# Gated linear attention: scores per head over 64 rows of TensorE instead of per pair with zero-padded queries

## The chip, the cores and the metric

The kernel runs on one NeuronCore of a Trainium2 chip. The metric is the device time of one execution, in microseconds, as the median of several runs. The program is one launch that computes two whole layers of a hybrid block, with nothing done on the host in between. It is written with a tile framework: the code allocates tiles from pools, and a scheduler in the build decides, from its own model of time, in which order the instructions stand on each engine, and which physical buffer each tile takes. On the chip the engines then run their fixed orders and wait for each other through semaphores.

## The reference, cut to what is touched

Each layer mixes tokens with three groups of heads (retention, gated linear attention, RWKV-7), projects the result, and runs a feed-forward network. The change concerns gated linear attention (GLA) alone: 4 heads, 48 key channels (padded to 64 in the kernel), 96 value channels, chunks of 64 tokens, in both directions over 1024 latent and 256 context tokens.

```python
def _gla_scan(seq, s0):
    """Chunked gated linear attention: S_n = diag(alpha_n) S_{n-1} + k_n^T v_n, o_n = q_n S_n."""
    causal = jnp.tril(jnp.ones((CHUNK, CHUNK), dtype=bool))

    def step(s, blk):
        qb, kb, vb, gb = blk
        cum = jnp.cumsum(gb, axis=2)
        rel = cum[:, :, :, None, :] - cum[:, :, None, :, :]
        decay = jnp.exp(jnp.where(causal[:, :, None], rel, -jnp.inf))
        sc = jnp.einsum("bhid,bhjd,bhijd->bhij", qb, kb, decay)
        o = jnp.einsum("bhij,bhjv->bhiv", sc, vb) + jnp.einsum("bhid,bhdv->bhiv", qb * jnp.exp(cum), s)
        ...
```

The score of a query i and a key j in one chunk carries a decay for every channel between i and j. The kernel does not form the array over (i, j, d). It splits the 64 x 64 square of a chunk into seven levels: the diagonal, and for block lengths 32, 16, 8, 4, 2 and 1 the pairs in the two halves of a block of twice that length. For a pair of one level the decay is a product of a factor of the query and a factor of the key, both measured from the middle of the block, so each level is one matrix product; masks put the levels together.

## The kernel before

Channels lie on partitions. A pair t of heads (t = 0, 1) fills the 128 partitions: head e of the pair has partitions 64e to 64e+63. The stage works on blocks n of 128 tokens (two chunks r = 0, 1), ten of them in layer 0 and eight in layer 1, and is the generator `gla` (L1063). For each block it yields once:

- `front(n+1)` (L1095) loads the next block: `gk` (keys), `gqz` (queries), `gvg` (values and gate), `glr`, and computes the log decays `glah` + `glal`. The queries are loaded zero-padded, by two transfers of half the partitions: `gqz` is [128, pair, 2, 128], and in its slot e only the partitions of head e hold queries; the others stay zero from a memset (L1078).
- `scores(n)` (L1116), for each pair t: for each chunk r two 512-wide decay exponents through PSUM tiles `pg` into `gEX` (L1132, ScalarE), then `gQT` (L1136, VectorE: the six levels' query factors times the padded queries, 768 wide), the keys' factors (L1138, GpSimd), `gqe` (L1139) and `gkh` (L1141) on VectorE. Then come the products: for each level and each chunk one matmul whose stationary operand is the keys of both heads (128 rows, 64 columns) and whose moving operand is the padded queries of both heads (128 wide). The padding keeps the heads apart. Chunk r writes the partitions 64r to 64r+63 of a PSUM tile. Levels (diagonal, 0, 1, 2) go to one bank, levels (3, 4, 5) to a second (L1143 to L1153). After each bank, VectorE puts its levels together into `gsc`: one product for the diagonal (L1156), one masked copy for each other level (L1158).
- `back(n)` (L1161) uses `gsc`, `gqe` and the states for the outputs, and updates the state `gSf` (L1013).

All these PSUM tiles have the tag `g1`, with GB = 4 banks; `back` has one more bank, `g2`. The names of the profile drop the bank number: both read as `pg`. In a row of the profile a matmul in float32 stands as two records, each with its own weight load: 14 score matmuls of a pair are 28 records, 4 of them named `pg<-gqz,gk` (the diagonal) and 24 named `pg<-gQT,gEX`.

Other work is interleaved with the blocks: the retention mixer (`rr`, `qx`, `mu`, `y`), the modulation matmuls whose weights `wmod` come by transfer (`pn`), and beside the last three blocks of a layer the output projection (`rw`). All transfers are issued from SP's queue (L246), all matmuls by L243.

Of the kernel before, what the change touches and what calls it, by code (L numbers as in the profile page):

```python
# [35 lines left out]
GB = 4  # L36
# [33 lines left out]
def rw_where(u):  # L70
    """block and chunk of either direction in step u"""
    ns = [(0, 1), (1, 0)][u // 2] if u < 4 else (u // 2, 11 - u // 2)
    return [(ns[0], u % 2), (ns[1], 1 - u % 2)]
# [96 lines left out]
class Kern:  # L170
# [77 lines left out]
    # ------------------------------------------------------------------ setup  # L248
# [34 lines left out]
    # per layer vectors, channel-major, and modulation  # L283
# [18 lines left out]
    def mod(self, l, V, p, parts, bufs):  # L302
        """parts: which sixths of the modulation (1024 columns each) to compute"""
# [27 lines left out]
    def mod_gain(self, l, V, part_scale, gname, add_one):  # L331
        """per-partition gain [128, 8, 2] = g * (scale + 1) or g * scale"""
# [11 lines left out]
    # ------------------------------------------------------------ norms  # L344
    def rstd(self, x, b, dst, pe=False):
        """dst [128, N] = (mean over channels of x^2 + 1e-6) ** -0.5 on all partitions; x [128, 8, N]; pe: the tensor
        engine sums over the channel tiles too"""
# [26 lines left out]
    def split_norm(self, x, b, A, B, s, xh, xl, pe=False):  # L374
        """xh + xl = x * rstd * A + B, x [128, 8, N]; A, B [128, 8, 2]"""
# [12 lines left out]
    def resid(self, f, b, gp, s, xsrc, xdst, pe=False):  # L388
        """f <- x + gp * f * rstd(f), in place; xsrc DRAM [128, 8, TOK], xdst also, or [128, 8, SEQ]"""
# [22 lines left out]
    # ------------------------------------------------------------ dense helpers  # L412
    def weights(self, p, segs, width):
        """segs: list of (dst offset, DRAM AP [1024, w]); returns lists of the hi and lo parts [128, width] per k tile"""
# [38 lines left out]
    # ------------------------------------------------------------ P1: RWKV columns  # L453
# [176 lines left out]
    def rw_heads(self, t, e):  # L630
        """the heads of parity e"""
        return t.rearrange("p (j e) x -> p e j x", e=2)[:, e]
# [10 lines left out]
    def rw_row(self, l, i, t, back=False):  # L643
        """row i of the operands, of all chunks, from t (or back into t)"""
# [5 lines left out]
    def rw_load(self, l, P, X, u):  # L650
        """operands of step u into X [128, 2, 9 or 15, 64], the decays into P; returns the inverse decay, kk and kk a of
        either direction"""
# [18 lines left out]
    def rw_decayed(self, dst, ops, P):  # L671
        """kk times the decay up to the token before"""
# [3 lines left out]
    def rw_inverses(self, l, p):  # L676
        """the triangular matrices of all steps, and the inverses of their diagonal blocks of 32 x 32"""
# [25 lines left out]
    def rw_inverse(self, l, bi):  # L703
        """minus the inverse of (identity + triangular), 96 matrices of 32 x 32, one per partition, in place; then the
        operands of the solves, [rows, (step, head), inverse | factors of its block off the diagonal]"""
# [21 lines left out]
    def silu(self, p, o, x):  # L727
        """o = x / (1 + exp(-x)) by Exp and Ln"""
# [8 lines left out]
    # ------------------------------------------------------------ P1: GLA and retention columns  # L737
# [64 lines left out]
    # ------------------------------------------------------------ retention mixer  # L802
    def ret(self, l, ctx_out, p):
# [18 lines left out]
        def rot(dst, src, n):  # L822
            """axial rotary over [128, 4, 2, 2, 16]"""
# [20 lines left out]
        def upd(d, new, old, kh, v):  # L844
            """new = decay * old + khat^T v, [128 (2 heads x 64), (2, 64)]"""
# [129 lines left out]
    # ------------------------------------------------------------ gated linear attention mixer  # L975
# [8 lines left out]
    def gla_logsig(self, p, ps):  # L984
        """log_sigmoid(ps), [128, n]"""
# [37 lines left out]
    def gla_state(self, l, p, C, d, n, bank, nb=2):  # L1023
        """k-hat (transposed) and per-chunk decays for direction d, block n"""
# [17 lines left out]
    def gla_back(self, l, p):  # L1042
        """states of the backward direction in front of every chunk"""
# [19 lines left out]
    def gla(self, l, ctx_out, p):  # L1063
# [16 lines left out]
        def early():  # L1080
            return self.pt("g1", GB)

# [12 lines left out]
        def front(n):  # L1095
# [4 lines left out]
            for e in range(2):  # L1100
                self.dma(qz[64 * e:64 * e + 64, :, e, :], self.QK[l][64 * e:64 * e + 64, 0:2, 128 * n:128 * n + 128])
# [640 lines left out]
```

## Time and profile before

| | |
|---|---|
| runs of the kernel before | 4218.07, 4218.18 and 4226.98 us, median 4218.18 |
| span of the profiled execution | 4221.6 us (no other time is given for that execution) |
| GLA stage, layer 0 / layer 1 | about 905 to 1225 us / 3125 to 3377 us of that span |
| TensorE, VectorE, ScalarE, GpSimd busy over the span | 93%, 56%, 39%, 41% |
| records of score matmuls | 864 + 144 = 1008 |

The profile page gives busy times, the span in 40 slices, and the chain of work that ended last. The trace behind it answers by tile, by line, by window and in order of time. A matmul's recorded duration holds the time in which it drains, so TensorE's busy share overstates its load; how many matmuls follow each other in what time tells more.

### The profile page before, as it was taken

To read this page: it belongs to the slowest core of one execution; us is meant where nothing else is said; L and a number is where in the kernel's file an instruction comes from. 1 tells how busy PE (TensorE), PEld (TensorE's weight loads), DVE (VectorE), ACT (ScalarE), POOL (GpSimd) and SP (SyncE) were. 2 spreads that over 40 slices of the span, in tenths; PEclk is the share of its full clock that TensorE was granted. 3 is DMA by queue.
4 is the path that set the end of the run, shared out by engine and by line. 5 is a ranking of instruction groups with operands and counts; after the bars stand their busy time and mean duration, and the time that the engine had idled before them with its cause. 6 is when DMAs were issued, how large, how long until landed. Compare 5 with 4: busy or idle time off the path is not lost. (4 is left out here: it accounts for less than half of the span.)

```text
span 4221.6 us, 74050 instructions
## 1 busy us (share of the span) xinstructions
PE 3927.3 (93%) x29094; PEld 3157.3 (75%) x29094; DVE 2346.4 (56%) x4053; ACT 1629.1 (39%) x3267; POOL 1730.6 (41%) x1686
## 2 busy tenths in 40 slices
PE   7998999899999999999998997999888979999998
PEld 3776888776677788888885675887856757888886
DVE  4565656658756633644445464666658565335444
ACT  4442334234435333522224443343244344334332
POOL 3155630323456544522223145640423465445443
PEclk8998999899999999999998998999989989999999
DMA  6586545665433333322222387554764253334332
GB/s 191 129 235 183 140 125 146 191 186 184 126 120 112 108 92 106 97 65 60 61 60 92 86 225 202 129 148 135 206 196 122 66 157 96 99 94 134 93 97 93
DMA packets 822655, 547.18 MB, mean 130 GB/s; under 512 B 317853, under 2 KB 727201, under 8 KB 822305
## 3 DMA queue, kind: packets, MB, share of 16 engines
q1 hardware_dynamic: 822016, 541.38, 44.9%
q8 instruction: 229, 3.75, 0.4%
q14 instruction: 122, 0.99, 0.1%
q0 software_dynamic: 288, 1.05, 0.1%
HBM read 421.96 MB, written 120.33 MB: 128 GB/s over the span
## 5 line engine op out<-in xcount | busy, mean ns | idle before, releaser
L243 PE MATMUL pd<-xh,whi 128*128 128x512 f32 (+1 forms) x2608 | 981.8, 377 | 30.8 <-ACT whi L433 13.9
L434 POOL TENSOR_TENSOR wlo<-wraw,whi 128x1024 fp32r<-128x1024 f32 (+1 forms) x328 | 678.4, 2072 | 786.8 <-ACT whi L433 652.2
L243 PE MATMUL pd<-xl,whi 128*128 128x512 f32 (+1 forms) x2608 | 987.7, 379 | 12.4 <-DVE xl L1437 4.6
L243 PE MATMUL pd<-xh,wlo 128*128 128x512 f32 (+1 forms) x2608 | 982.5, 377 | 15.7 <-POOL wlo L434 15.7
L243 PEld LDWEIGHTS pd<-xh,whi 128*128 128x128 f32 x2608 | 500.3, 192 | 135.1 <-DVE xh L384 18.8
L243 PEld LDWEIGHTS pd<-xl,whi 128*128 128x128 f32 x2608 | 500.5, 192 | 122.9 <-issue 13.4
L243 PEld LDWEIGHTS pd<-xh,wlo 128*128 128x128 f32 x2608 | 500.6, 192 | 118.3 <-POOL wlo L434 20.5
L433 ACT CAST whi<-wraw 128x1024 fp32r<-128x1024 f32 (+1 forms) x328 | 289.2, 891 | 483.1 <-PE pd L243 266.9
L1517 DVE TENSOR_TENSOR f<-pm,f 128x512 f32<-128x512 f32 (+1 forms) x400 | 247.2, 635 | 354.1 <-PE pm L243 354.1
L1503 POOL TENSOR_TENSOR dl<-draw,dh 128x512 fp32r<-128x512 f32 x176 | 242.6, 1378 | 480.2 <-ACT dh L1502 450.8
L243 PE MATMUL pm<-hl,dh 128*128 128x512 f32 (+1 forms) x880 | 327.6, 373 | 8.1 <-DVE hl L1492 8.1
L243 PE MATMUL pm<-hh,dh 128*128 128x512 f32 (+1 forms) x880 | 322.3, 374 | 9.4 <-DVE f L1517 3.9
L243 PE MATMUL pd<-whi,xh 128*128 128x256 f32 x1072 | 317.6, 297 | 1.9 <-DVE st L438 1.9
L243 PE MATMUL pm<-hh,dl 128*128 128x512 f32 (+1 forms) x880 | 318.2, 372 | 0.0
L243 PE MATMUL pd<-wlo,xh 128*128 128x256 f32 x1072 | 317.8, 297 | 0.0
L243 PE MATMUL pd<-whi,xl 128*128 128x256 f32 x1072 | 317.7, 297 | 0.0
L1502 ACT CAST dh<-draw 128x512 fp32r<-128x512 f32 x176 | 109.1, 620 | 456.7 <-DMA draw<-in_w_ffn_down 245.1
L236 ACT ACTIVATE silu<-silu 128x512 f32<-128x512 f32 (+2 forms) x332 | 171.7, 517 | 191.9 <-DVE silu L731 185.7
L243 PEld LDWEIGHTS pd<-whi,xh 128*128 128x128 f32 x1072 | 213.2, 199 | 8.9 <-issue 3.2
L243 PEld LDWEIGHTS pd<-wlo,xh 128*128 128x128 f32 x1072 | 214.1, 200 | 7.1 <-issue 5.4
L243 PEld LDWEIGHTS pd<-whi,xl 128*128 128x128 f32 x1072 | 213.5, 199 | 7.2 <-issue 5.0
L1492 DVE TENSOR_TENSOR hl<-sg,hh 128x512 fp32r<-128x512 f32 (+1 forms) x110 | 179.5, 1632 | 57.1 <-ACT hh L1491 57.1
(296 smaller groups left out, 7161.2 us busy)
## 6 DMA issues: line engine op xcount, KB each, us to landing
wmod<-in_w_mod SPq DMA_DIRECT2D x192, 256.0 KB
draw<-in_w_ffn_down SPq DMA_DIRECT2D x176, 256.0 KB
wraw<-in_w_ffn_gate SPq DMA_DIRECT2D x88, 512.0 KB
wraw<-in_w_ffn_up SPq DMA_DIRECT2D x88, 512.0 KB
wraw<-in_w_in SPq DMA_DIRECT2D x100, 256.0 KB
a<-ops SPq DMA_DIRECT2D x80, 288.0 KB
X<-ops SPq DMA_DIRECT2D x36, 480.0 KB
wraw<-in_w_out SPq DMA_DIRECT2D x32, 512.0 KB
```

The source lines that it names most:

```text
L236: i = self.nc.scalar.activation(out, in_, f, bias=bias, scale=scale)
L243: return self.nc.tensor.matmul(out, l, r, start=start, stop=stop)
L433: nc.scalar.copy(wh[i][:, :, w], r)
L434: nc.gpsimd.tensor_tensor(wl[i][:, :, w], r, wh[i][:, :, w].bitcast(F32), op=ALU.subtract)
L1492: nc.vector.tensor_tensor(hl[q][b], sg, hh[q][b].bitcast(F32), op=ALU.subtract)
L1502: nc.scalar.copy(dh[:, w], raw)
L1503: nc.gpsimd.tensor_tensor(dl[:, w], raw, dh[:, w].bitcast(F32), op=ALU.subtract)
L1517: nc.vector.tensor_tensor(facc[b][:, m, :], ps[:, :n], facc[b][:, m, :], op=ALU.add)
```

## The change

The scores are computed per head, over 64 rows of TensorE. The queries are loaded a second time, unpadded, as `gq` ([128, pair, 128], one more transfer a block, 128 KB). `gQT` is built from them and is 384 wide instead of 768. Each level and chunk takes two matmuls, one for each head, with 64 rows, 64 stationary and 64 moving columns; the heads lie on the two row halves of the array, the chunks on the two column halves. All seven levels of a pair go into one PSUM tile of two banks (tag `gs`, one buffer), head e in bank e, and VectorE reads each level across both banks. `g1` keeps two banks. `gqz` stays for `gqe`.

```diff
-GB = 4
+GB = 2
...
+            qc = self.t(p, [128, 2, 128], "gq", bufs=2)
+            self.dma(qc, self.QK[l][:, 0:2, 128 * n:128 * n + 128])
...
-                    QT[r] = qt = self.t(p, [128, 6, 2, 64], "gQT", bufs=4)
+                    QT[r] = qt = self.t(p, [128, 6, 64], "gQT", bufs=4)
...
-                    nc.vector.tensor_tensor(qt, ex[:, 0:6, :].unsqueeze(2).to_broadcast([128, 6, 2, 64]),
-                                            q.to_broadcast([128, 6, 2, 64]), op=ALU.mult)
+                    nc.vector.tensor_tensor(qt, ex[:, 0:6, :], qc[:, t, tk].unsqueeze(1).to_broadcast([128, 6, 64]), op=ALU.mult)
...
-                for levels in ((6, 0, 1, 2), (3, 4, 5)):
-                    ps = early()
-                    p4 = ps.rearrange("p (a e x) -> p a e x", a=4, e=2)
-                    for a, li in enumerate(levels):
+                ps = self.psum.tile([128, 2, 512], F32, tag="gs", name=self.nm("pgs"), bufs=1)
+                for li in (6, 0, 1, 2, 3, 4, 5):
+                    at = slice(64 * (li + 1) % 448, 64 * (li + 1) % 448 + 64)
+                    for e in range(2):
+                        R = slice(64 * e, 64 * e + 64)
                         for r in range(2):
                             tk = slice(64 * r, 64 * r + 64)
                             if li == 6:
-                                kl, ql = kc[:, t, tk], qz[:, t, :, tk]
+                                kl, ql = kc[R, t, tk], qc[R, t, tk]
                             else:
-                                kl, ql = EX[r][:, 6 + li, :], QT[r][:, li]
-                            self.mm(p4[64 * r:64 * r + 64, a], kl, ql)
-                    for a, li in enumerate(levels):
-                        if li == 6:
-                            nc.vector.tensor_tensor(sct, p4[:, a], gdiag.unsqueeze(1).to_broadcast([128, 2, 64]), op=ALU.mult)
-                        else:
-                            nc.vector.copy_predicated(sct, gmask[:, li, :].unsqueeze(1).to_broadcast([128, 2, 64]), p4[:, a])
+                                kl, ql = EX[r][R, 6 + li, :], QT[r][R, li]
+                            self.mm(ps[64 * r:64 * r + 64, e, at], kl, ql)
+                for li in (6, 0, 1, 2, 3, 4, 5):
+                    x = ps[:, :, 64 * (li + 1) % 448:64 * (li + 1) % 448 + 64]
+                    if li == 6:
+                        nc.vector.tensor_tensor(sct, x, gdiag.unsqueeze(1).to_broadcast([128, 2, 64]), op=ALU.mult)
+                    else:
+                        nc.vector.copy_predicated(sct, gmask[:, li, :].unsqueeze(1).to_broadcast([128, 2, 64]), x)
```

On TensorE, in the fourth block of layer 0, the second pair's scores begin like this before (tiles 2084 and 2085 are the pair's two banks, 2086 the transposed keys, 11982 and 11997 the query factors of the two chunks):

```order
L243 MATMUL pn_12255<-wmod_12300,silc_120 2x256 x2
L243 MATMUL pg_2084_12011<-gqz_1721_10584,gk_11471 64x128 x2
L243 MATMUL pg_2084_12011<-gQT_11982,gEX_11981 64x128
L243 MATMUL pg_2085_12024<-gQT_11982,gEX_11981 64x128
L1018 MATMUL pg_2086_12034<-ident_67,gkh_11924 128x128
L243 MATMUL pg_2084_12011<-gQT_11997,gEX_11996 64x128
```

Nine more of them follow, then the other transpose. In the same place of the program now (2083 holds the transposed keys, the tile `pgs` both banks, 12083 and 12098 are the query factors):

```order
L1018 MATMUL pg_2083_12148<-ident_67,gkh_12012 128x128
L243 MATMUL pn_12369<-wmod_12406,silc_120 2x256
L243 MATMUL pn_12369<-wmod_12410,silc_120 2x256 x2
L243 MATMUL pn_12369<-wmod_12414,silc_120 2x256
L243 MATMUL pgs_12112<-gq_11533,gk_11529 64x64 x4
L243 MATMUL pgs_12112<-gQT_12083,gEX_12082 64x64
L243 MATMUL pgs_12112<-gQT_12098,gEX_12097 64x64
```

Twenty-two more follow without a break, alternating between the chunks, so that the group now stands in one piece and behind both transposes.

On VectorE, at the same place, the reads of the first pair's second bank (2075) end and those of the second pair's first bank (2084) begin like this before:

```order
L956 TENSOR_TENSOR y_11775<-y_11775,va_11779 128x256
L1158 COPY_PREDICATED gsc_11925<-gmask_10571,pg_2075_11971 128x128
L958 TENSOR_TENSOR y_11775<-y_11775,gt_11722 128x256
L1158 COPY_PREDICATED gsc_11925<-gmask_10571,pg_2075_11971 128x128
L1156 TENSOR_TENSOR gsc_11925<-pg_2084_12011,gdiag_10573 128x128
L1158 COPY_PREDICATED gsc_11925<-gmask_10571,pg_2084_12011 128x128 x3
```

Now (`pgs_12046` is the first pair's tile, `pgs_12112` the second's):

```order
L1161 COPY_PREDICATED gsc_12013<-gmask_10571,pgs_12046 128x128 x2
L945 TENSOR_REDUCE mu_12240<-rr_12218 128x4
L854 SCALAR_TENSOR_TENSOR Sf_1485_9379<-Sf_1486_9380,rcd_9373,rr_12233 128x64 x2
L840 TENSOR_TENSOR khat_12342<-kr_12340,rkd_9369 128x256
L946 TENSOR_SCALAR mu_12240<-mu_12240 128x4
L949 TENSOR_TENSOR y_12243<-rr_12218,mu_12240 128x256
L953 TENSOR_REDUCE va_12247<-sq_12245 128x4
L956 TENSOR_TENSOR y_12243<-y_12243,va_12247 128x256
L1159 TENSOR_TENSOR gsc_12013<-pgs_12112,gdiag_10573 128x128
```

Seven rows of the retention mixer, eight instructions, now stand between the last read of the first pair's tile and the first read of the second's.

## Rows read from the trace of the kernel before

**Rows 1.** The page: busy time of each engine; TensorE's granted clock in 40 slices.
```profile
PE 3927.3 (93%) x29094; PEld 3157.3 (75%) x29094; DVE 2346.4 (56%) x4053; ACT 1629.1 (39%) x3267; POOL 1730.6 (41%) x1686
PEclk8998999899999999999998998999989989999999
```

**Rows 2.** Windows: the two stages; busy us and instructions by engine, clock, DMA.
```profile
core 0: us, PE busy (x) PEld busy (x) DVE busy (x) ACT busy (x) POOL busy (x), PEclk, DMA share, GB/s
905.00:1225.00 320.00, 302.51 (x2452) 217.76 (x2451) 222.22 (x486) 139.18 (x338) 125.85 (x113) 0.95 0.46 139
3125.00:3377.00 252.00, 228.64 (x1784) 165.55 (x1776) 178.67 (x363) 106.98 (x248) 101.43 (x82) 0.96 0.37 110
```

**Rows 3.** The chain that ended last, 3194 to 3378 us: shares; pieces (start, us).
```profile
by line: PE pg L243 36.4%; PE rw L243 20.8%; DVE gkh L1141 6.5%; DVE gqe L1139 5.5%; DVE gQT L1136 5.4%; DMA f<-yt 2.6%; issue 2.5%; DVE gsc L1158 2.5%; PE rr L243 2.5%; DVE xl L1437 2.1%; PE pg L1018 1.6%; DVE qx L909 1.2%; DVE gy L1197 1.
...
3225.13 0.96 DVE gQT L1136
...
3231.84 2.75 PE pg L243 x20
```

**Rows 4.** Groups by line and shape: count | busy us, mean ns | idle before.
```profile
L243 PE MATMUL pg<-gQT,gEX 128*64 128x128 f32 x864 | 83.3, 295 | 10.3 <-DVE gQT L1136 5.0 <-POOL gEX L1138 5.0
L243 PE MATMUL pg<-gqz,gk 128*64 128x128 f32 x144 | 16.0, 301 | 0.8 <-ACT gEX L236 0.8
L1136 DVE TENSOR_TENSOR gQT<-gEX,gqz 128x768 f32<-128x768 f32 x72 | 81.5, 1132 | 20.6 <-ACT gEX L236 20.2 <-issue 0.2
L1139 DVE TENSOR_TENSOR gqe<-gEX,gqz 128x256 f32<-128x256 f32 x72 | 58.9, 818 | 4.5 <-ACT gEX L236 4.2
L1256 DVE TENSOR_TENSOR AR<-X,P 128x384 f32<-128x384 f32 x36 | 24.3, 674 | 0.0
L1402 DVE TENSOR_TENSOR fo<-fo,fmu 128x384 f32<-128x384 f32 x18 | 12.9, 719 | 0.3
L243 PE MATMUL ra<-SAV,SA 64*64 64x64 f32 x960 | 48.0, 229 | 3.4 <-DVE SA L635 3.4
L243 PE MATMUL rd<-XE 32*32 32x32 f32 x960 | 23.7, 196 | 1.3 <-DMA XE<-xe 1.3
L243 PE MATMUL pg<-gvg,gkhT 64*64 64x96 f32 x272 | 12.7, 263 | 0.0
```

**Rows 5.** TensorE in order of time, the fourth block: start, us for all, count.
```profile
1019.41 1.48 PE L243 MATMUL pg<-gQT,gEX 128*64 128x128 f32 x20
...
1022.92 0.44 PE L243 MATMUL pg<-gqz,gk 128*64 128x128 f32 x4
...
1024.64 1.52 PE L243 MATMUL pg<-gQT,gEX 128*64 128x128 f32 x20 [0.58 <-POOL gEX L1138]
```

**Rows 6.** TensorE in order of time: runs of small matmuls on parts of the array.
```profile
1029.31 0.57 PE L243 MATMUL pg<-gvg,gkhT 64*64 64x96 f32 x16
...
474.36 0.80 PE L243 MATMUL ra<-SAV,SA 64*64 64x64 f32 x20
...
459.14 0.57 PE L243 MATMUL rd<-XE 32*32 32x32 f32 x24
```

**Rows 7.** VectorE and GpSimd in order of time, the first block.
```profile
920.29 0.95 DVE L1136 TENSOR_TENSOR gQT<-gEX,gqz 128x768 f32<-128x768 f32 x1
920.48 1.61 POOL L1138 TENSOR_TENSOR gEX<-gEX,gk 128x384 f32<-128x384 f32 x1 [0.40 <-ACT gEX L236]
...
921.16 1.22 DVE L1139 TENSOR_TENSOR gqe<-gEX,gqz 128x256 f32<-128x256 f32 x1
```

**Rows 8.** VectorE in order of time, the fourth block: reads of the score banks.
```profile
1021.16 0.28 DVE L1156 TENSOR_TENSOR gsc<-pg,gdiag 128x128 f32<-128x128 f32 x1
...
1025.79 0.29 DVE L1158 COPY_PREDICATED gsc<-gmask,pg 128x128 f32<-128x128 int32 x1
1025.99 0.28 DVE L1156 TENSOR_TENSOR gsc<-pg,gdiag 128x128 f32<-128x128 f32 x1
```

**Rows 9.** SP's issues by tile: ns min/median/max; transfers of the stage, layer 0.
```profile
L246 SPq DMA_DIRECT2D gk<-qk x40: 359/382/1416, 365.7 to 3298.3; - x40
...
gk<-qk SPq DMA_DIRECT2D x10, 128.0 KB
```

**Rows 10.** Windows: three single blocks, columns as in rows 2.
```profile
1009.60:1036.70 27.10, 26.49 (x242) 17.89 (x242) 20.50 (x49) 12.21 (x31) 8.85 (x9) 1.00 0.64 199
...
1158.70:1186.40 27.70, 27.70 (x218) 22.90 (x219) 17.56 (x33) 11.65 (x26) 12.49 (x8) 1.00 0.19 52
...
3245.30:3280.50 35.20, 23.05 (x164) 16.13 (x165) 26.80 (x38) 15.85 (x34) 21.49 (x14) 0.81 0.43 117
```

More of the change, by code (lines that the diff above doesn't have):

```diff
@@ L1113, in front @@
             nc.gpsimd.tensor_tensor(lal, la, lah.bitcast(F32), op=ALU.subtract)
-            B[n] = kc, qz, vg, lah, lal
+            B[n] = kc, qz, qc, vg, lah, lal
         def scores(n):
-            kc, qz, vg, lah, lal = B[n]
+            kc, qz, qc, vg, lah, lal = B[n]
             kh = self.t(p, [128, 2, 128], "gkh", bufs=2)
```

## The prediction

> **What bounds the kernel now.** I read the page first, then the windows of the stage that the change touches, the chain that ended last, the groups by shape, and single stretches in order of time. Over the whole span TensorE is busy 93%, and its clock stands near full speed [rows 1]. That is an average; the change touches only the GLA stage, so the question is what that stage waits for. It takes 320 us in layer 0 and 252 us in layer 1, 572 us in all, 18 blocks. There TensorE is busy 302.5 and 228.6 us, 93% of the time, VectorE 222.2 and 178.7 us, 70%; ScalarE and GpSimd have slack, and the transfers take 0.46 and 0.37 of the queues [rows 2]. TensorE's share hides drain times, so the chain matters more. From 3194 to 3378 us it runs over TensorE for 36.4 + 20.8 + 2.5 + 1.6 = 61.3% of the time and over VectorE for most of the rest; gQT alone has 5.4%, and single score groups and gQT products stand in it [rows 3]. The path goes back and forth between these two engines, and the change makes work on both smaller. The chain was followed only through layer 1's stage; for layer 0 I assume the same shares, since its busy shares are alike [rows 2].
>
> **The change, part by part.**
>
> *Score matmuls on TensorE.* Before, there are 864 + 144 = 1008 records [rows 4]. A run of 20 takes 1.48 or 1.52 us [rows 5]; less the last one's own 0.295 us [rows 4] that is 1.185 / 19 to 1.225 / 19, about 63.5 ns each. 1008 x 63.5 ns = 64.0 us. After, there are twice as many, 2016, each 64 wide on a quarter of the array. The trace before has no such run of exactly this shape, but neighbours on both sides. The state updates (gkhT) use two row halves and two column halves in one run, as the new scores do, with 96 columns: 16 in 0.57 us, less 0.263 us, over 15 is 20.5 ns; scaled to 64 columns 13.6 ns. The RWKV matmuls (ra) have the new shape but use only two of the four quarters: (0.80 - 0.229) / 19 = 30.1 ns. The 32-wide ones (rd) come every (0.57 - 0.196) / 23 = 16.3 ns [rows 4, 6]. I take 18 ns, between the scaled and the unscaled four-quarter run, the nearest row: 2016 x 18 = 36.3 us, so 27.7 us less. The bounds: 13.6 ns gives 36.6 us less, 30.1 ns only 3.3 us less. Of TensorE's time 61.3% lies on the path, so I count 27.7 x 0.613 = 17.0 us.
>
> The rd run shows starts 16.3 ns apart on average. The Trainium skill, "TensorE: Matmul & The Clock Gate", section "Wait — 56ns, not 53.3ns?", says that start-to-start never drops below about 25 ns however small a matmul is, which speaks against splitting a matmul in two. By it the sum, as an estimate, would be 2016 x 25 = 50.4 us, 13.6 us less, 8.3 us on the path, and the time 4202 us. The row has less than that floor, so the trace does not agree where matmuls run on different parts of the array.
>
> *gQT on VectorE.* 72 products of 768 columns average 1132 ns; other products of 384 columns average 674 and 719 ns, about 697 [rows 4]. 72 x 435 ns = 31.3 us less. A lower bound: on the line between gqe's 818 ns at 256 columns and 1132 at 768, 384 columns cost 896 ns, which saves 17.0 us. Could gqe just wait longer and take the gain back? GpSimd's product starts 0.19 us after gQT starts and ends 0.85 us after gQT ended [rows 7]; gqe ends 0.29 us after that product. The three follow one another, so a shorter gQT moves all three forward, and I leave that bound out. On the chain gQT has 5.4% of 184 us, 9.9 us [rows 3]; the six blocks there hold 24 of them, 24 x 1.132 = 27.2 us, so 36% is on the path: 31.3 x 0.36 = 11.3 us.
>
> *One score tile instead of rotating banks.* Before, the second pair's matmuls could run while VectorE still read the first pair's banks. In the fourth block they start at 1022.92 [rows 5], the last read of the first pair ends at 1026.08, and the second pair's first read starts at 1025.99 [rows 8]; in 7 of the 18 blocks the reads follow each other like that, within 0.1 us. Now the second pair's 56 records must wait for the last read, and VectorE for them: 56 x 18 ns + 0.229 us = 1.24 us. Behind the waiting matmul stand in TensorE's queue the second pair's own scores, then `back`'s products; behind VectorE's wait its other work, some of which the new order puts into the gap (the second pair of order excerpts). I charge the 7 blocks at the share by which VectorE's products lie on the path: 7 x 1.24 x 0.36 = 3.1 us lost. The bounds are 0 and 18 x 1.24 = 22 us. The exponents lose two of four banks, but no longer share them with scores; I cost that at nothing, covered by ScalarE's slack [rows 2].
>
> *The rest.* VectorE's 252 reads keep their number and their 128 columns, now in two banks; no row shows such a read. I take no change; if each cost as much as two reads of 0.28 us, it would be 71 us of VectorE's time, 25 us on the path. The transfer of gq adds 18 issues of about 0.38 us on SP, like gk's [rows 9]; ahead of gvg's and all later issues it adds 6.9 us over 572 us, and 128 KB each to queues less than half used [rows 2]. Its buffer comes free when gk's does. Nothing while that cover lasts, 7 us without it.
>
> *Sum.* 17.0 + 11.3 - 3.1 = 25.2 us less. The profiled span, 4221.6 us, would be 4196; it lies 3.4 us above the median of the runs, 4218.18, from which I forecast: **4193 us**. Its own range, from the bounds of the single terms, is about 4180 to 4206.
>
> **The rivals.**
>
> *The row halves do not overlap*, so the change does not do what it says: 30.1 ns a record, 3.3 x 0.613 = 2.0 us from TensorE, 2.0 + 11.3 - 3.1 = 10 us less: 4208 us. Against it stands the gkhT run, closer than two quarters allow [rows 6].
>
> *Both savings lie on the path in full.* TensorE and VectorE take turns and each waits for the other: 27.7 + 31.3 - 3.1 = 56 us less: 4162 us. For it: the chain is a long alternation; against it: both engines have other work to fill in.
>
> *The gain is hidden.* A block takes 27.1 us where VectorE works 20.5 us of it beside the modulation, and 27.7 us where VectorE works 17.6 us beside the output projection [rows 10]; if something common sets that period, such as the recurrence through states and buffers, nothing comes off: 4218 us. Against it: TensorE is full in both blocks.
>
> *A matmul start floor.* If small matmuls cannot start closer than the unscaled 20.5 ns, the TensorE term is (64.0 - 41.3) x 0.613 = 13.9 us, and the time 4196, inside the forecast's range. The page's floor, weighed above, would give the 4202 us that stand there.
>
> *Slower: TensorE's queue stands at the second pair's scores.* The place is the first matmul into the single score tile. Before, it started 3.2 us before the first pair's last read ended (1022.92 against 1026.08). If VectorE's reads drag as long as they do now and the order places nothing in between, TensorE stands 3.2 us a block, 18 x 3.2 = 57 us, against 28 us gained: 4218 + 57 - 28 = 4247 us. It decides from 28.3 / 18 = 1.6 us a block. For it: such a stand also lowers the clock; in the block at 3245 us TensorE is busy only 23 of 35.2 us and the mean granted clock is 0.81 of 2.4 GHz, so part of it went at 1.2 GHz [rows 10]. Against it: the new order puts both transposes and modulation matmuls ahead of these scores.
>
> **How the numbers follow.** The forecast has 0.52, the floor 0.04, halves without overlap 0.09, both savings in full 0.08, the hidden gain 0.13, the standing queue 0.14. About 0.2%, 8.4 us, is what a measurement of this kernel can tell from no change. Faster: 0.52 + 0.04 + 0.08 and two thirds of the 0.09, 0.70. Within 0.2%: the rest of the 0.09 and 0.13, 0.16. Slower: 0.14. The range 4164 to 4222 holds all but the standing queue and most of the full savings, and takes in the bounds of each term alone except the doubled reads.
>
> **What would show it.** Right: 2016 score records in runs of 46 to 56 at 14 to 20 ns each; gQT at about 0.7 us; blocks some 1.4 us shorter on average; the second pair's first read about 1.2 us after the first pair's last. Wrong: score runs at 30 ns each; gqe or gkh longer by what gQT lost; waits of TensorE for gsc of over 1.6 us in most blocks; a lower clock in the stage; reads of gsc clearly longer than 0.3 us; or a change of time outside the two stages, where the order of some in-projection matmuls beside the RWKV steps of layer 1 has moved too.

## The result and the profile after

The changed kernel takes 4256.28 us (4251.73 to 4257.64), 1.0085 times the kernel before, with a 95% interval of 1.007 to 1.0099: 38 us slower, where 25 us less was forecast. Its profiled execution took 4254.93 us; the span is 4252.6 us, 31.0 above before's.

The page, TensorE's busy time and granted clock, to be read beside [rows 1]:

```profile
PE 3911.4 (92%) x30102; PEld 3137.1 (74%) x30102; DVE 2305.5 (54%) x4053; ACT 1634.9 (38%) x3267; POOL 1718.7 (40%) x1686
PEclk8998999989989999999998998999987889999999
```

TensorE's records grew by 1008 and its busy time fell; VectorE's fell by 40.9 us. So the work was saved. The two GLA stages, in windows as in [rows 2]:

```profile
core 0: us, PE busy (x) PEld busy (x) DVE busy (x) ACT busy (x) POOL busy (x), PEclk, DMA share, GB/s
905.00:1260.00 355.00, 314.13 (x3128) 222.92 (x3128) 209.55 (x494) 148.39 (x349) 127.37 (x120) 0.91 0.46 141
3140.00:3409.00 269.00, 231.98 (x2204) 168.05 (x2203) 155.88 (x359) 107.99 (x247) 97.29 (x81) 0.86 0.35 106
```

Layer 0's stage is 35 us longer and layer 1's 17 us. Of the 35, about half (16 to 20 us, by where the stage is taken to end) comes back behind the stage, where the output projection had already run ahead: 384 records of `rw` lie in the window of layer 0's stage, 274 before. From the last `gsq` of layer 1 to the end both kernels take the same 848 us. TensorE's mean clock fell from 0.95 and 0.96 to 0.91 and 0.86 of 2.4 GHz. With the two levels of 2.4 and 1.2 GHz this means that 18% and 28% of the stages went at 1.2 GHz, where it had been 10% and 8%.

The matmuls, gQT and the reads came out as planned. Groups by line and shape, as in [rows 4] (count | busy us, mean ns | idle before):

```profile
L1138 DVE TENSOR_TENSOR gQT<-gEX,gq 128x384 f32<-128x384 f32 x72 | 48.7, 677 | 26.4 <-ACT gEX L236 26.1
L1140 DVE TENSOR_TENSOR gqe<-gEX,gqz 128x256 f32<-128x256 f32 x72 | 52.0, 722 | 24.7 <-ACT gEX L236 23.0 <-DMA glr<-lrg 0.9 <-issue 0.7
L243 PE MATMUL pgs<-gQT,gEX 64*64 64x64 f32 x1728 | 43.5, 239 | 2.9 <-POOL gEX L1139 2.8
L1161 DVE COPY_PREDICATED gsc<-gmask,pgs 128x128 f32<-128x128 int32 x216 | 64.6, 299 | 5.2
```

VectorE's saving was not all gain: ahead of gQT and gqe it waited 24.4 us for the exponents before (20.2 + 4.2, [rows 4]) and waits 49.1 us now (26.1 + 23.0).

What got longer is the block. TensorE in order of time, layer 0, before (start, us for all, operation, count; `glev` are the exponent products, two records for each 512-wide bank):

```profile
1040.01 0.48 PE L243 MATMUL pg<-glev,glah 128*128 128x512 f32 x1
1040.33 0.40 PE L243 MATMUL pg<-glev,glal 128*128 128x512 f32 x1
...
1041.51 0.40 PE L243 MATMUL pg<-glev,glah 128*128 128x512 f32 x1
1041.74 0.40 PE L243 MATMUL pg<-glev,glal 128*128 128x512 f32 x1
1041.97 0.49 PE L1200 MATMUL pg<-ident,gy 128*128 128x128 f32 x3
```

The first pair's four exponents fill four banks in one go, 2.1 us. The same place after:

```profile
1043.45 2.12 PE L243 MATMUL pn<-wmod,silc 128*2 128x256 f32 x8 [2.10 <-DMA wmod<-in_w_mod]
...
1055.18 0.51 PE L243 MATMUL pg<-glev,glah 128*128 128x512 f32 x1
...
1055.99 0.40 PE L243 MATMUL pg<-glev,glal 128*128 128x512 f32 x1
1056.22 0.33 PE L243 MATMUL rr<-v,sc 128*128 128x64 f32 x2
...
1058.94 0.45 PE L243 MATMUL rr<-v,khat 128*64 128x64 f32 x8
1059.32 0.50 PE L243 MATMUL pg<-glev,glah 128*128 128x512 f32 x1
...
1060.13 0.40 PE L243 MATMUL pg<-glev,glal 128*128 128x512 f32 x1
...
1063.61 0.92 PE L243 MATMUL pgs<-gQT,gEX 64*64 64x64 f32 x46
...
1069.09 0.44 PE L1018 MATMUL pg<-ident,gkh 128*128 128x128 f32 x2
1070.85 0.60 PE L243 MATMUL pn<-wmod,silc 128*2 128x256 f32 x4 [1.32 <-DMA wmod<-in_w_mod]
1071.38 0.34 PE L243 MATMUL pgs<-gq,gk 64*64 64x64 f32 x8
1071.55 0.88 PE L243 MATMUL pgs<-gQT,gEX 64*64 64x64 f32 x48
```

Two exponents fill both banks; the retention products stand in between, and the other two exponents follow 4.1 us after the first two: 5.4 us for the pair instead of 2.1. This is one block, and one in which the kernel before was at its best: over all 18 blocks, from the start of a first pair's first exponent on ScalarE to the end of its fourth, the mean is 5.9 us before and 6.6 after, and for second pairs 5.9 and 5.7. What the mean of the blocks lost comes further down. The second pair's scores come 7.8 us after the first pair's, behind the transposes and a wait for modulation weights. VectorE at the second pair:

```profile
1069.05 0.63 DVE L1161 COPY_PREDICATED gsc<-gmask,pgs 128x128 f32<-128x128 int32 x2
1069.71 1.43 DVE L909 TENSOR_TENSOR qx<-rqz,rqd 128x512 f32<-128x512 f32 x2
1072.50 0.29 DVE L1159 TENSOR_TENSOR gsc<-pgs,gdiag 128x128 f32<-128x128 f32 x1 [1.35 <-PE pgs L243]
```

The last read of the first pair ends at 1069.68 and the second pair's first read starts at 1072.50, a gap of 2.8 us, where [rows 8] had them touch.

The granted clock fell behind such a stand (a time in which TensorE has nothing to do). The first row of TensorE's above comes after one of 2.10 us; windows of that stand, of the work behind it and of the time after that, columns as above:

```profile
1041.30:1043.40 2.10, 0.06 (x1) 0.00 (x0) 2.06 (x8) 0.00 (x0) 0.00 (x0) 1.00 0.75 220
1043.45:1046.90 3.45, 3.37 (x14) 1.33 (x14) 0.31 (x2) 0.37 (x1) 0.00 (x0) 0.51 0.89 293
1046.95:1050.00 3.05, 3.05 (x27) 1.52 (x27) 2.11 (x6) 2.37 (x7) 0.96 (x2) 1.00 0.88 283
```

In the window behind the stand the granted clock was 0.51, so nearly all of it went at 1.2 GHz; in the next it was 1.00, 2.4 GHz.

ScalarE shows how far the next block's exponents run ahead: how long before the end of a block the next one has begun. `gsq` is the square at the end of a block. Before:

```profile
1003.83 0.60 ACT L236 ACTIVATE gEX<-pg 128x512 f32<-128x512 f32 x1 [0.43 <-PE pg L243]
1009.60 0.49 ACT L236 ACTIVATE gsq<-pg 128x384 f32<-128x384 f32 x1 [2.52 <-PE pg L243]
```

After:

```profile
1053.33 0.49 ACT L236 ACTIVATE gsq<-pg 128x384 f32<-128x384 f32 x1 [1.30 <-PE pg L243]
1056.02 1.08 ACT L236 ACTIVATE gEX<-pg 128x512 f32<-128x512 f32 x2 [1.69 <-PE pg L243]
```

Such a run-ahead is found in 8 of the 16 intervals between blocks of one layer before, and in 3 of 16 after. The table takes the marks (first exponent, first and last read of each pair's scores into `gsc`, `gsq`) in all blocks, and the mean over these 16 intervals. A block's period, from the start of one `gsq` to the next, then falls into the stretches below; "gap" is from the last read of the first pair to the first read of the second. The kernels below the second row are experiments of the next section; in the first column a minus sign is the run-ahead.

| us | `gsq` to next block's first exponent | to the first read | first pair's reads | gap | second pair's reads | to `gsq` | period |
|---|---|---|---|---|---|---|---|
| before | -1.0 | 13.4 | 5.5 | 2.4 | 3.1 | 6.8 | 30.1 |
| after | 1.3 | 13.3 | 3.9 | 3.8 | 2.9 | 7.6 | 32.7 |
| b_rb1 | -0.7 | 14.5 | 4.9 | 2.2 | 3.4 | 6.7 | 31.0 |
| e6_exps_two_banks | 1.5 | 14.1 | 4.9 | 1.7 | 3.6 | 6.8 | 32.5 |
| e1_psum_alone | -6.5 | 15.8 | 7.9 | 3.6 | 6.9 | 7.0 | 34.6 |
| e15_rb1 | -0.8 | 15.2 | 3.8 | 4.0 | 3.4 | 7.2 | 32.9 |
| e3_gb3_rb1 | -8.0 | 18.6 | 4.0 | 3.9 | 3.5 | 7.6 | 29.6 |
| e12_padded_gb3 | -16.6 | 19.8 | 7.4 | 3.8 | 8.5 | 7.1 | 30.0 |

After against before: the reads are 1.8 us shorter, the start is 2.2 us later (first two columns), the gap 1.4 longer, the end 0.85 longer; 2.6 us a block more.

### The profile page after: what moved, and what is told of

Read it like the earlier page. It is cut to its first block, busy times and chain, and to the rows that moved or that the text cites. A ratio compares the mean times of both kernels' runs of the same rounds, so it can differ in the third digit from the quotient of the medians.

```text
span 4252.6 us, 76033 instructions
## 1 busy us (share of the span) xinstructions
PE 3911.4 (92%) x30102; PEld 3137.1 (74%) x30102; DVE 2305.5 (54%) x4053; ACT 1634.9 (38%) x3267; POOL 1718.7 (40%) x1686
```

## The experiments

Three theories stood at the start. **1, banks**: the accumulator layout (two rotating banks instead of four, one two-bank score tile) loses more than the smaller work gives; 1a blames the exponents' two banks, 1b the single tile. **2, clock**: TensorE has less to do and is granted less clock. **3, transfer**: the additional queries on SP's queue delay the modulation weights. Ratios are to the kernel before, measured together with each run, with 95% intervals. The last column is from the profiled execution alone: the time from the first read into `gsc` to the last `gsq` of a layer, both layers together, and the time between the two.

| run | layout: rotating + scores + retention | score work | us | ratio | blocks, between |
|---|---|---|---|---|---|
| before | 4 shared + 2 | padded | 4216 to 4220 | 1 | 520, 1922 |
| b_rb1 | 4 shared + 1 | padded | 4234.73 | 1.0036 (1.0017 to 1.0055) | 531, 1916 |
| e6_exps_two_banks | 2 + 2 single + 2 | padded | 4250.42 | 1.0085 (1.0053 to 1.0117) | 564, 1908 |
| e1_psum_alone | 2 + one double + 2 | padded | 4300.18 | 1.02 (1.0174 to 1.0225) | 623, 1898 |
| e12_padded_gb3 | 3 + one double + 1 | padded | 4235.22 | 1.004 (1.0021 to 1.0058) | 534, 1914 |
| after | 2 + one double + 2 | per head | 4256.28 | 1.0085 (1.007 to 1.0099) | 563, 1906 |
| e15_rb1 | 2 + one double + 1 | per head | 4239.63 | 1.0051 (1.0031 to 1.0071) | 565, 1895 |
| e3_gb3_rb1 | 3 + one double + 1 | per head | 4219.14 | 1.0012 (0.9994 to 1.003) | 506, 1926 |

### The layout alone

```diff
-GB = 4
+GB = 2
...
-                for levels in ((6, 0, 1, 2), (3, 4, 5)):
-                    ps = early()
-                    p4 = ps.rearrange("p (a e x) -> p a e x", a=4, e=2)
+                pg = self.psum.tile([128, 2, 512], F32, tag="gs", name=self.nm("pgs"), bufs=1)
+                for b, levels in enumerate(((6, 0, 1, 2), (3, 4, 5))):
+                    p4 = pg[:, b].rearrange("p (a e x) -> p a e x", a=4, e=2)
```

> The kernel before, with its padded matmuls and 768-wide gQT, but with the changed kernel's layout of the accumulator banks alone: two rotating banks for exponents, transposes and updates, and one two-bank tile for a pair's scores. If the banks cost the time (theory 1): everything that the layout loses and nothing of what the smaller matmuls give, so 4256 us or more, up to some 4290. If the clock falls because the score work became shorter (theory 2): 4218 within 10 us, since the work is as long as before. If the additional transfer of the queries on SP's queue costs it (theory 3): 4218 within 10 us, since there is none here.

It took 4300 us, 2.0% more than before, and 10 us more than the upper end of what theory 1 expected. Its two stages:

```profile
905.00:1297.00 392.00, 343.03 (x2547) 243.13 (x2543) 225.15 (x487) 147.12 (x345) 132.15 (x116) 0.86 0.39 120
3172.00:3449.00 277.00, 240.50 (x1767) 169.70 (x1760) 163.83 (x357) 108.53 (x247) 100.70 (x82) 0.89 0.34 102
```

With the old score work and no added transfer the layout loses 82 us, and the clock falls as well. Theory 1 holds; 2 and 3 are not needed for it. The smaller work then gives 44 us back (4300 to 4256), more than the 28 that the prediction counted. TensorE waits for modulation weights here too, 9.3 us in layer 0's stage, so these waits come without the added transfer.

Next, the exponents' banks apart from the single tile: two rotating banks, but scores in two one-bank tiles of their own (`ps = self.pt("gs", 2)`, GB = 2).

> The kernel before with its padded matmuls; the exponents, transposes and updates have two rotating banks, and the scores two one-bank tiles of their own, which rotate: a score bank comes free after its own three or four reads. Of the layout's two parts only the smaller number of banks for the exponents is kept, not the single two-bank tile. If the banks of the exponents cost the time (theory 1a): near the run of the whole layout, 4280 to 4300 us. If the wait for the single score tile costs it (theory 1b): 4216 to 4235 us.

It took 4250 us, between the two expectations: 32 us for the rotating banks, and 50 us more for putting both score banks into one tile that comes free only after the last read. Both 1a and 1b have their part. The table of stretches shows where: with the exponents' banks taken away (e6) a block's first read comes 15.6 us behind the last `gsq` instead of 12.4 (the first two columns), and nothing else got clearly longer. With the single tile as well (e1) the blocks even run ahead, by 6.5 us, but the reads of the two pairs and the gap take 18.4 us instead of 10.2.

### A third rotating bank, with its controls

`GB = 3`, `RB = 1` on the changed kernel, on the kernel with the padded work (e12), and the lost retention bank alone (`RB = 1`) on before and on the changed kernel:

> The changed kernel with three rotating banks instead of two for exponents, transposes and updates; the third is taken from the retention mixer, which keeps one of its two. Theory 1 (too few banks): 4240 us or less, unless the retention mixer loses as much by its bank. Theory 2 (clock) and theory 3 (transfer): 4256 us or more.

> The kernel before with one bank instead of two for the retention mixer, and one of the eight banks unused: the control for the changed kernel with three rotating banks. If the retention mixer needs its second bank, 4225 us or more, and the third rotating bank is worth more than the 37 us that were measured; if not, 4216 us within 8 us.

> The changed kernel with one bank for the retention mixer and the other unused: the control for three rotating banks. If the retention mixer loses as much here as in the kernel before (15 us): about 4271 us, and the third rotating bank alone is worth about 52 us. If it loses nothing here, since other things are waited for: 4256 us within 6 us, and the third bank is worth 37 us.

> The kernel before with its padded matmuls and wide gQT, in the layout of the run at 4219 us: three rotating banks, one two-bank score tile, one retention bank. The difference to that run is what the narrow matmuls and gQT are worth in this layout. If they are worth the 28 us that the prediction counted: 4247 us within 10. If as much as with two rotating banks, where they gave 44 us: 4263 us within 10. If the score tile is not waited for once a third bank is there, less than 4235 us.

The third bank brings the changed kernel to 4219 us, level with before. The retention bank alone costs the kernel before 15 us (0.36%) and makes the changed one 17 us faster, which none of the theories had; so of the 37 us, 20 are the third bank's (4240 to 4219). The padded work with three banks takes 4235 us, as much as before with one retention bank: **with three rotating banks the changed layout costs nothing that can be measured** (each ratio is known to 0.2%), and neither does the single score tile in it; with two rotating banks that tile cost 50 us. And the smaller work is worth 16 us there (4235 to 4219) instead of 44. Differences of 15 to 20 us are near what an unrelated edit moved in another run (15 us, below), so these are rough.

The last column of the table of runs says more, for one execution each. From the changed kernel to e15 the blocks stay as long as they were (563 and 565 us), and the gain, 11 us in these executions, lies between the two stages: it is not a gain of the GLA blocks. From e15 to e3 the blocks get 58 us shorter, and 31 of these are lost again between the stages. From e12 to e3, the smaller work with three banks, the blocks get 27 us shorter and the rest 11 longer. A time of the whole program therefore understates here what a bank or a matmul is worth in the stage.

The table of stretches shows why in the pair that differs by one bank, e15 and e3: the run-ahead grows from 0.8 to 8.0 us, the period falls from 32.9 to 29.6, and no other stretch but the one to the first read changes by over 0.5 us. In ScalarE's rows of the kernel with three banks:

```profile
1019.65 0.60 ACT L236 ACTIVATE gEX<-pg 128x512 f32<-128x512 f32 x1 [0.46 <-PE pg L243]
1024.63 0.60 ACT L236 ACTIVATE gEX<-pg 128x512 f32<-128x512 f32 x1 [2.39 <-PE pg L243]
1031.68 0.49 ACT L236 ACTIVATE gsq<-pg 128x384 f32<-128x384 f32 x1 [2.66 <-PE pg L243]
```

Two exponents of the next block start 7 us and more before the block ends. In e12 the reads are drawn out as in e1 (7.4 and 8.5 us), but the next block's exponents start 16.6 us ahead, and the period stays at 30.0.

### The parts of the smaller work, and the transfer

gQT 768 wide again, all else as changed (`QT[r][R, li, e]` for the matmuls):

> The changed kernel, with its banks, its 64-row matmuls and its transfer, but gQT is built from the padded queries, 768 wide, as before. It parts the 44 us by which the changed kernel lies below the run of its layout with the padded matmuls (4300 against 4256). If the prediction's shares hold (17.0 us for the matmuls, 11.3 us for gQT), gQT undone costs some 40% of 44 us: 4267 to 4274 us. If nearly all of gQT's 31 us lies on the path: 4280 us or more. If gQT is off the path: 4256 us within 5 us.

It took 4252.53 us, 1.0082 (1.0062 to 1.0103): no more than the changed kernel, though gQT costs 37 us more:

```profile
L1138 DVE TENSOR_TENSOR gQT<-gEX,gqz 128x768 f32<-128x768 f32 x72 | 86.1, 1196 | 27.7 <-ACT gEX L236 27.3
```

So in this layout no gain of the narrower gQT can be seen, and what the smaller work gives comes from the matmuls.

The transfer, taken away (two ScalarE copies from `gqz` instead), and added alone to the kernel before:

> The changed kernel, but the unpadded queries are not loaded by a transfer: ScalarE copies them from the padded ones, two copies a block of 64 partitions x 256 elements. Theory 3 (the transfer on SP's queue holds up the modulation weights in layer 0): at least 20 us below the changed kernel, 4236 us or less. Theories 1 and 2: within 5 us of 4256 us.

> The kernel before with the additional transfer of the unpadded queries alone: 18 more issues on SP's queue and 18 x 128 KB, which nothing reads. Theory 3: 14 us or more above 4218, as the changed kernel gained 14 us without it. The prediction's term: 0, at most 7 us: 4218 to 4225 us.

Without it 4242.34 us, 1.0066 (1.0041 to 1.0091), 14 us less and between the two expectations; alone 4222.49 us, 1.001 (0.9995 to 1.0025), 4 us more. The two disagree; the second measures the transfer by itself, in the order of the kernel before, and theory 3 fails there. Whether it costs up to 14 us in the changed order stays open; the 82 us of e1 were lost without it.

### The clock, and the waits for weights

Each score matmul twice:

> The changed kernel, with each of the score matmuls issued twice into the same place: 2016 more records, about 28 us of TensorE's time at 14 ns each, which make the score bursts as long again as they were before the change. If the clock falls because TensorE has less to do (theory 2), the mean granted clock in the two stages rises from 0.91 and 0.86 towards 0.95, which is worth up to 42 us against the 28 us added: 4242 to 4256 us. If the clock only follows the waits (theory 1): the clock within 0.02 of the changed kernel's, and the time 4262 to 4284 us.

It took 4297.71 us, 1.0186 (1.0156 to 1.0216), 41 us more than the changed kernel and more than either expectation. Its stages:

```profile
905.00:1271.00 366.00, 328.10 (x4230) 243.54 (x4230) 208.59 (x487) 146.08 (x345) 127.14 (x116) 0.91 0.43 133
3158.00:3455.00 297.00, 251.57 (x3096) 183.88 (x3095) 157.82 (x356) 108.51 (x248) 96.44 (x81) 0.86 0.32 97
```

The clock stayed at 0.91 and 0.86 with twice the score work, and e1, with all of the old score work, had 0.86 and 0.89. Theory 2 falls: lighter score work did not lower it. The time rose by more than the added work's 28 us. That fits bursts that lie on the path in full when there are two banks; what the other 13 us are is not shown.

Six buffers for the modulation weights, on the changed kernel and on the version v1 below (`self.mod(ll, self.V[ll], pmod, [m], 6)`):

> The changed kernel with six buffers instead of four for the modulation's weights, so that SP may issue them earlier. If TensorE's waits for these weights, 12.5 + 4.8 us in the two stages of the changed kernel against 0.4 us before, are time lost: 4238 to 4246 us. If they only show that modulation matmuls were moved into gaps that the banks leave (theory 1): 4250 us or more.

> Three rotating banks, no padded queries, and six buffers for the modulation's weights. If the waits for those weights are time lost there as well: 4195 to 4203 us; if not, 4208 us within 6 us.

4259.27 us, 1.01 (1.0068 to 1.0132), and 4223.06 us, 1.0019 (0.9996 to 1.0042): nothing gained, and 15 us lost on v1, outside both of its expectations. But the waits themselves hardly shrank, in layer 0's stage from 12.5 to 10.1 us and on v1 from 7.5 to 5.2, so these two runs do not test what the waits cost. Other runs speak against them as the cause: e12 has 7.4 us of them there and b_rb1 0.7, at the same time within 1 us, and the run without the transfer (e2) has 16.2 and is faster than the changed kernel. That they are a sign of the order, in which modulation matmuls fill what the banks leave, is the reading that fits; it is not shown. The 15 us are also a warning: an edit beside the matter moves the build's order and the time by as much, so differences below some 17 us, e2's and e15's too, cannot be put down to one cause here.

### Other ways to share the banks

One rotating bank for each head, four shared, and VectorE reads each head by itself (`ps = [early() for e in range(2)]`, GB = 4):

> The changed kernel's 64-row matmuls, but a pair's scores go to one rotating bank for each head, out of four shared with exponents, transposes and updates, as the kernel before shares them; VectorE then reads each head by itself, 504 reads of 64 columns instead of 252 of 128. Theory 1: the banks' loss comes back and the smaller matmuls' gain stays, but 252 more reads of some 0.15 to 0.25 us cost VectorE 38 to 63 us, about 36% of it on the path, 14 to 23 us: 4205 to 4235 us. Theory 2 (clock) and theory 3 (transfer): 4256 us or more, plus the reads, 4270 us or more.

4238.88 us, 1.0045 (1.0022 to 1.0067), just above theory 1's 4205 to 4235 us. The 504 reads take 0.22 us each on average; that they cost much of what the banks bring is likely, but was not tested apart. The Trainium skill, "TensorEngine Tiling (Array Packing)", section "Gotcha 1: PSUM Pressure", says that different row tiles write to different banks, which raises the pressure on them. The 82 us are the price of the layout that was chosen here, measured with the old matmuls. Whether the two heads' matmuls could share a bank at once was not tried.

Two two-bank tiles that everything rotates through:

> The changed kernel with two two-bank tiles that everything shares in rotation: both halves of an exponent in one tile (one 1024-wide Exp instead of two of 512), a pair's scores in one, the transposes in one, both updates in one. Theory 1a (too few banks for the exponents): the four banks are shared as in the kernel before, so 4190 to 4215 us if two large tiles serve as well as four small ones; about 4256 us if what counts is the number of tiles that can be open at once. Theory 1b (a single score tile): a second tile is there, 4190 to 4215 us. Theory 2 (clock): 4256 us.

4245.52 us, 1.0081 (1.005 to 1.0113). Four banks, but only two open tiles: the run-ahead is gone (first exponent 4.1 us after `gsq` on average). That is nearer to the 4256 us expected if the number of tiles counts that can be open at once than to the 4190 to 4215 us expected if the banks count. It points to the open tiles and does not prove it, since the run also widens the exponents and gives two banks to work that needs one.

Version v1: three rotating banks, one retention bank, and `gqe` built per head from the unpadded queries, so that `gqz` and its two transfers go:

```diff
...
-                    nc.vector.tensor_tensor(qe[:, r, t], ex[:, 12:14, :].unsqueeze(2).to_broadcast([128, 2, 2, 64]),
-                                            q.to_broadcast([128, 2, 2, 64]), op=ALU.mult)
+                    for e in range(2):
+                        R = slice(64 * e, 64 * e + 64)
+                        nc.vector.tensor_tensor(qe[R, r, t, :, e, :], ex[R, 12:14, :],
+                                                qc[R, t, tk].unsqueeze(1).to_broadcast([64, 2, 64]), op=ALU.mult)
...
```

> The changed kernel with three rotating banks (one from the retention mixer), and without the padded queries: gqe's two tiles are zeroed once, and VectorE writes each head's half from the unpadded queries, 144 products of 64 x 128 in place of 72 of 128 x 256; two of the three query transfers a block go. Theory 1 (banks alone): 4219 us as with three banks, or less by what VectorE saves, down to some 4205. Theory 3 with theory 1 (the issues on SP cost too): as much again as the transfer that was taken away had cost, 14 us or more, 4205 us or less.

4207.78 us, 0.9975 (0.9956 to 0.9994): faster than both kernels, by 0.25% against before; this is 12 us against the kernel before of the same measurement, again less than the 17 us. Its variants take the third bank, or a fourth, from `back` (`late()` returns `early()`), or put the transposed keys into `back`'s bank:

> As the kernel with three rotating banks and without padded queries, but the third bank is the one that `back` had for itself, and the retention mixer keeps its two: the outputs and their transposes rotate through the three banks too. If the 15 us that the kernel before lost with one retention bank come back, and the outputs do not hold their bank too long: 4190 to 4200 us. If a bank that the outputs hold for long is as bad as one too few: 4220 us or more.

> As the kernel with three rotating banks and without padded queries, with a fourth rotating bank, the one that `back` had for itself; the retention mixer has one. The number of rotating banks of the kernel before and the single score tile: if the rotating banks are what was missing, 4190 to 4208 us; if the outputs hold theirs too long, 4220 us or more.

> The kernel at 4208 us (three rotating banks, no padded queries), with the transposed keys in the bank of the outputs instead of a rotating one. If a rotating bank less in demand counts (theory 1): 4195 to 4205 us. If the outputs' bank, which then is asked for three times a block, is waited for: 4215 us or more.

4297.92 us, 1.0198 (1.0172 to 1.0225); 4296.6 us, 1.0187 (1.0163 to 1.021); 4230.72 us, 1.0036 (1.0022 to 1.005). `back` keeps its outputs in a bank from the first product to `gy`; in the rotation that is worse than a bank too few, even with four. In both of the slow ones the next block's first exponent comes 7.7 to 7.8 us behind `gsq` in the mean, where v1's comes 8.2 us ahead of it.

## Why the prediction was wrong

- **The step that failed** is the sentence on the exponents: "The exponents lose two of four banks, but no longer share them with scores; I cost that at nothing, covered by ScalarE's slack". The slack was ScalarE's, but what ran short was places for TensorE to write to ahead of time. By itself that step measured 32 us (e6; 22 to 49 by its interval), where the range had no bound for it at all. In the blocks it is a start that comes 3.2 us later. One bank more for the same work (e15 to e3) takes the run-ahead from 0.8 to 8.0 us. The rows to look at were there: ScalarE's exponents before a block's `gsq` (1003.83 against 1009.60 above) show a block in which the next one has begun.
- **The single score tile** was charged at 3.1 us with a bound of 22. With two rotating banks it measured 50 us (e6 to e1); in the changed kernel the gap grew by 1.4 us in the mean of all blocks, 25 us, not by 1.24 us in seven of them. (Counted in the trace before, the reads follow each other within 0.1 us in six blocks, not seven; that changes the term by less than half a us.) With three rotating banks it cost nothing that can be measured (e12 against b_rb1). The price was not a term of its own: it depends on the number of rotating banks beside the tile. Together the two layout terms measured 82 us (e1), where 3.1 were counted; the smaller work gave 44 of these back, which leaves the 38.
- **The score matmuls** ran as foreseen: 46 in 0.92 us, less 0.239 us, over 45 is 15 ns, where 18 was taken. But the two terms of 17.0 and 11.3 us measured 16 together with three banks (e12 to e3), and the matmuls alone 48 with two (e1 to e13); shares of the chain before do not hold once the limit moves. The 61.3% also held the output projection, 20.8%, in which the scores have no part.
- **gQT** got its duration, 677 ns against the 697 taken, but not its value: 11.3 us were counted, and undoing it cost nothing (e13). VectorE's share of the chain was no share of what a shorter product gives; it then waits for the exponents (49.1 us ahead of gQT and gqe, 24.4 before).
- **The transfer** (0 to 7 us) measured 4 us by itself (e11), within the noise; reads across two banks 299 ns, where [rows 8] had 0.28 to 0.30 us: both right.
- **The slower rival** gave 4247 us, near the result, by luck, since its mechanism is not there: TensorE waits for `gsc` ahead of the scores 2.0 us in layer 0's whole stage, not 1.6 us a block. The order filled the place, as the prediction's argument against the rival said; but the transposes and modulation matmuls that it put there delay the scores themselves. Of its signs the lower clock came, though not from less score work, as the scores issued twice show.

No wait names the banks. TensorE's waits of 2 us and more in layer 0's stage, after (total us, times, longest us):

```profile
PE pn L243 <- DMA wmod<-in_w_mod: 12.5, 14, 2.1
PE pg L1203 <- DVE gy L1200: 8.5, 2, 5.3
PE pg L1018 <- DVE gkh L1142: 2.5, 3, 0.9
PE pgs L243 <- POOL gEX L1139: 2.3, 1, 2.3
PE pgs L243 <- DVE gsc L1161: 2.0, 2, 1.5
```

The longest in layer 1's stage is another, the wait of the transposes for `gkh`, which took 0.8 us before:

```profile
PE pg L1018 <- DVE gkh L1142: 14.1, 6, 3.9
```

Which wait carries the loss differs from layer to layer; that the order brings all of them is argued, not shown.

Open: why one retention bank less helps the changed kernel between the stages and harms the one before, and how much of each difference under 17 us is the build's order.

## What to carry to other kernels

When an edit takes accumulator banks from a producer, ask what the producer starts early today and what that hides; idle time of the engine that empties the banks says nothing about it. Put a price on the layout by building it alone, with the old work: here that one run (82 us) would have decided. Look at the stage and at the whole program apart: here half of what a stage gained could be lost behind it. Where a build orders the work, count the tiles that can be open, and hold differences under what an unrelated edit moves (here up to 17 us) for unexplained.

## What the runs showed of the hardware

The records of float32 matmuls of 64 x 64 on the four quarters of the array (two records to a matmul) followed each other every 14 to 15 ns on average (48 in 0.88 us, less 0.239 us, over 47 is 13.6 ns). That is below the start-to-start floor of about 25 ns of the Trainium skill, "TensorE: Matmul & The Clock Gate", section "Wait — 56ns, not 53.3ns?", further than the 16.3 ns of the run before [rows 6]. That counts records; a whole float32 matmul of two records takes 27 ns, and where records are what the floor means, the measurement decides. The granted clock did not follow the amount of work: doubled score bursts left it at 0.91 and 0.86.
